# First feed-forward of a hybrid transformer layer, context rows: where the latent rows are asked for, how many weight pieces are under way, and where the position sums stand

## The chip, the cores and the metric

The program runs on one core of one Trainium2 chip. The metric is the device time of one execution in microseconds, a median of three runs. Five engines take part, each with its own stream of instructions that runs in order: TensorE (PE: matrix products; its weight loads are listed as PEld), VectorE (DVE), ScalarE (ACT), GpSimd (POOL) and SyncE (SP), whose queue asks for all the transfers between DRAM and SBUF that are spoken of here. An instruction that waits holds up everything behind it on its engine.

## The reference, cut to what matters

One layer over 1024 latent rows and 256 context rows of width 1024, all in float32. Both streams go through the same first feed-forward with their own shift, scale and gate; latents have grid positions added first:

```python
h = x + grid_pos_emb(rows)          # latents, 1024 rows
hc = ctx                            # context, 256 rows

def ffn_sublayer(h, shift, scale, gate, g, w_in, w_out):
    hn = modulate(rmsnorm(h, g), shift, scale)
    a, b = jnp.split(hn @ w_in, 2, axis=-1)      # w_in (1024, 2 * 2816)
    y = (jax.nn.silu(a) * b) @ w_out
    return h + 0.5 * gate[:, None, :] * y

h  = ffn_sublayer(h,  mods[0],   mods[1],   mods[2],   g_ffn1, w_ffn1_in, w_ffn1_out)
hc = ffn_sublayer(hc, mods_c[0], mods_c[1], mods_c[2], g_ffn1, w_ffn1_in, w_ffn1_out)
```

Behind it come a combined projection, a two-way recurrent mixing, a gating branch, a second feed-forward and a last norm. The change touches none of these.

## The kernel before, in words

Every float32 product is made of three: each operand is split into a rounded part (ACT, a cast) and the remainder (DVE, a subtraction), and PE adds up high·high, high·low and low·high.

The stage of interest is the first product of the context rows. The input weights `w1i` come as 44 pieces of 128 x 1024 (512 KB), two for each of the NF = 22 column groups f: piece 2f for `a`, 2f + 1 for `b`. PE works through a piece in 24 matmuls (8 slices of the width, 3 products each; listed as `pa` and `pb`, `L195`). After each odd f, four instructions make the gated product of two groups: silu on ACT (`sil`, `L1134`), the product with `pb` on DVE (`L1140`), a cast on ACT (`gc`, `L1142`) and the remainder on DVE (`L1143`); two stores put it away (`gcsp`, `L1145`).

Class `Weights` runs the pieces. `fetch()` asks for the next one into a `raw` tile (`L131`): of four in a row two use a pair of tiles of their own, and two use pages of a larger set. `load()` splits the oldest one asked for into an `hl` tile (cast `L158` on ACT, subtraction `L159` on DVE) and then asks for one more. There are five `hl` tiles, so a piece can be split only when PE is done with the piece five earlier. Eight pieces are asked for before the stage; `W.asked` is the newest.

Beside it the same loop prepares the latents for the stage behind it. They come as 16 tiles `h[tb][d]` of 128 x 512 (256 KB; two halves tb, eight slices d), asked for at `L1103`, two in each f from 1 to 8. For f from 2 to 9 the positions are added on DVE (`add_pos`, `L901`), and the squares are taken on ACT (`L219` for the first of each half, `L222`) and summed on DVE (`acc`, `L223`). At f = 10 come the norm of the latents (sums over the width on PE, `L228`; an inverse root in small DVE instructions, `L788` to `L800`; a diagonal, `L238` and `L239`; its broadcast on PE, `rb`, `L244`), then scaling in place (`L275` on DVE, `L276` on ACT) and splits of the scaled tiles (`fa`, later `fb` and `fc`, with differences at `L328`). From f = 13 on, weights of the next stage are asked for as well (`rawh`, `L385`) and summed (`L392`, `L393`). The next stage is a product of the latents with the same weights in seven-product form (`Gate`; PE `L429`, weights split into `ring` tiles).

Side work of this sort isn't issued where it is written: it is put into a list `todo` (`slow` does this with a price), and `pump`, called after each group of three matmuls, takes entries from it as credit allows.

A scheduler orders what is traced: it puts the instructions of each engine into one order when the program is built, by dependencies and its own idea of durations. `tc.issue_after(x)` binds what is traced inside it to stand behind instruction x if both are on the same engine. It makes no wait on the chip; it only fixes order. `behind(fn, ins)` wraps a function in such bounds. In the kernel before, each piece is asked for behind the one before it, and the rows of `h` behind `W.asked`, the newest piece asked for when the loop is at that f. The transfers that SP asks for also take turns with eight completion marks, so that one asked for waits until the one eight earlier has landed.

Of the kernel before, what the change touches and what calls it, by code (L numbers as in the profile page):

```python
# [55 lines left out]
def _build(ctx, tc, nc, a, out):  # L56
# [50 lines left out]
    class Weights:  # L107


        def __init__(self, order, name):  # L110
            self.c = ExitStack()
            self.pool = self.c.enter_context(tc.tile_pool(name=name, bufs=1, reuse_waits="tile"))
            self.order = deque(order)
            self.ready = deque()
            self.raws = deque()
            self.asked = None
            self.held = 0
            self.n = 0

        def fetch(self):  # L120
            n, i, w = self.order.popleft()
            src = a[n][i]
            if self.n % 4 < 2:
                raw = self.pool.tile([128, w], F32, name="raw", tag="raw", bufs=2)
            else:
                raw = hnp.tile([128, w], F32, name="raw", tag="pg1", bufs=8)
            self.n += 1
            with ExitStack() as es:
                if self.asked is not None:
                    es.enter_context(tc.issue_after(self.asked.ins))  # L130
                self.asked = nc.sync.dma_start(raw, src)  # L131
            self.raws.append((n, i, w, raw))

        def load(self):
            if not self.raws:
                self.fetch()
            n, i, w, raw = self.raws.popleft()
            hl = self.pool.tile([128, 2, w], F32R, name="hl", tag="hl", bufs=5)
            split(hl, raw)
            self.ready.append((n, i, hl))  # L140
            self.held += 1
            if self.order:
                self.fetch()

        def take(self, n, i):
# [11 lines left out]
    def split(hl, src):  # L157
        hi = S.copy(hl[:, 0, :], src)  # L158
        return hi, V.tensor_sub(hl[:, 1, :], src, hl[:, 0, :].bitcast(F32))  # L159

    def behind(fn, ins):

        def run():
            with ExitStack() as es:
                for i in ins:
                    es.enter_context(tc.issue_after(i.ins))
                fn()

        run.cost = COST(fn)
        return run  # L170
# [723 lines left out]
    def add_pos(tb, d, h=h, pos=pos):  # L894
        hv = h[tb][d].rearrange("p (r c) -> p r c", c=64)
        if d < 4:
            pv = pos[:, d * 16 + tb * 8:d * 16 + tb * 8 + 8].unsqueeze(2).to_broadcast([128, 8, 64])
        else:
            o = 64 + (d - 4) * 64
            pv = pos[:, o:o + 64].unsqueeze(1).to_broadcast([128, 8, 64])  # L900
        V.tensor_tensor(hv, hv, pv, ALU.add)  # L901
# [192 lines left out]
    def slow(fn, *args, cost=1024):  # L1094
        f = it(fn, *args)
        f.cost = cost
        todo.append(f)

    for f in range(1, NF):
        if f <= NKT:  # L1100
            with tc.issue_after(W.asked.ins):
                for tb in range(2):
                    nc.sync.dma_start(h[tb][f - 1], a["xT"][f - 1, :, tb * 512:(tb + 1) * 512])  # L1103
        if 2 <= f < 2 + NKT:
            if f - 2 < len(SIDE):
                slow(side, *SIDE[f - 2], 0)
            for tb in range(2):
                slow(add_pos, tb, f - 2)
                slow(n1[tb].sq, f - 2)
        if f == 2 + NKT:  # L1110
            todo.extend([n1[0].rstd, nop, n1[1].rstd, nop, n1[0].bcast, n1[1].bcast])
            for d in range(NKT):
                slow(n1[0].inplace, d, s0, b0)
                slow(A.F.early, fpage, 1 if d < 4 else 2, d % 4)
            for d in range(NKT):
                slow(n1[1].inplace, d, s0, b0)
        if f == 12:
            A.head()
        if f > 12:
            with tc.issue_after(W.asked.ins):  # L1120
                A.preload()
        if f == 1:
            pa, pb = pab
        else:
            if f % 2 == 0:
                pa, pb = mm_ps("pa"), mm_ps("pb")
            for pt, i in ((pa, 0), (pb, 1)):
                proj(pt[:, f % 2 * 256:f % 2 * 256 + 256], W.take("w1i", 2 * f + i), hnc, f % 2 == 0)
                W.done()
        if f % 2 == 0:  # L1130
            continue
        with ExitStack() as es:
            sil = t2("sil")
            S.activation(sil, pa, AF.Silu)  # L1134
            if f == NF - 1:
                flush()
                W.c.close()
                A.begin()
                es.enter_context(tc.issue_after(A.q.last[1].ins))
            V.tensor_mul(sil, sil, pb)  # L1140
            g = [t2("gc", F32R) for _ in range(2)]
            S.copy(g[0], sil)  # L1142
            V.tensor_sub(g[1], sil, g[0].bitcast(F32))  # L1143
        for y in range(2):
            nc.sync.dma_start(gcsp[f // 2, y].rearrange("p f c -> p (f c)"), g[y].bitcast(F32))  # L1145
# [1353 lines left out]
```

## Time and profile before

| what | value |
|---|---|
| median of 3 runs | 2636.53 us (2634.86 to 2637.92) |
| the profiled execution: its own time, its span | 2635.57 us, 2633.8 us |
| PE busy in the span | 2614.7 us (99%) |
| DVE, ACT, POOL busy | 1976.6 us (75%), 1206.5 us (46%), 75.0 us (3%) |
| granted TensorE clock | 0.998 |
| transfers | 449.07 MB, mean 171 GB/s |

The span runs from the first to the last instruction; 1.77 us of the execution's own time lie outside it. Matmuls overlap in the profile, so a busy PE says that it was never without work, not that it could do no more. The stage that the change touches lies between about 24 us (first matmul of the context product) and 161.7 us (the last one); the latents' product follows at once. In a row of the waits stand the waiting engine and line, who ended the wait, the total in us, how often, and the longest.

### The profile page before, as it was taken

How to read it: one execution, taken by the hardware profiler on the slowest of the kernel's cores; microseconds unless marked ns; L12 is line 12 of the kernel's file. 1: busy time of each engine (PE TensorE's matmuls, PEld its weight loads, DVE VectorE, ACT ScalarE, POOL GpSimd, SP SyncE). 2: the span in 40 equal slices, each digit the busy share in tenths (PEclk: the TensorE clock that was granted, in tenths of full speed). 3: DMA queues.
4: the chain of work that ended last, by engine and by line, in shares of the span. 5: the costliest groups of instructions: out<-in, count | busy, mean ns of one | idle time of the engine just before them, and what ended most of it. 6: DMA issues, size and time to landing. Idle time of an engine off the chain costs nothing.

```text
span 2633.8 us, 36017 instructions
## 1 busy us (share of the span) xinstructions
PE 2614.7 (99%) x12930; PEld 2214.2 (84%) x12930; DVE 1976.6 (75%) x3529; ACT 1206.5 (46%) x2170; POOL 75.0 (3%) x158
## 2 busy tenths in 40 slices
PE   9999999999999999999999999999999999999998
PEld 9988888888889878888888888888887888888887
DVE  6989678687989646787674878778799766665855
ACT  5754444444347525564443454333346444344433
POOL 0000000000000000000000002221000000000000
PEclk9999999999999999999999999999999999999999
DMA  9734345368577122256553566446441333337644
GB/s 341 267 137 146 125 150 175 124 234 301 177 268 264 66 80 92 104 187 194 191 184 104 172 205 237 162 154 203 136 150 47 128 136 124 112 125 281 200 159 179
DMA packets 192691, 449.07 MB, mean 171 GB/s; under 512 B 20096, under 2 KB 44160, under 8 KB 192512
## 3 DMA queue, kind: packets, MB, share of 16 engines
q1 hardware_dynamic: 192080, 446.38, 49.6%
q8 instruction: 102, 1.67, 0.3%
q14 instruction: 77, 0.63, 0.1%
q10 hardware_dynamic: 432, 0.39, 0.0%
HBM read 325.44 MB, written 121.32 MB: 170 GB/s over the span
## 4 chain that ended last, share of the span: by engine, by line
PE 91%; DMA 4%; DVE 2%; issue 2%; ACT 1%; SPq 0%; POOL 0%; POOLq 0%; ACTq 0%; DVEq 0%
PE qa L429 18%; PE pq L1462 17%; PE po L553 14%; PE qb L429 13%; PE pt L1946 6%; PE pr L1381 6%; PE po L2320 3%; PE pc L1248 2%; PE pn L2106 2%; PE pb L195 2%; PE pa L195 1%; PE pu L1782 1%; PE pkc L1441 1%; PE pn L2104 1%; PE pvc L1538 1%
## 5 line engine op out<-in xcount | busy, mean ns | idle before, releaser
L159 DVE TENSOR_TENSOR ring<-rawq,ring 128x512 fp32r<-128x512 f32 x408 | 280.9, 689 | 221.7 <-ACT ring L158 219.6
L553 PE MATMUL po<-gring,wring 128*128 128x512 f32 (+1 forms) x1896 | 423.5, 384 | 0.0
L553 PEld LDWEIGHTS po<-gring,wring 128*128 128x128 f32 x1896 | 349.5, 188 | 70.0
L158 ACT CAST ring<-rawq 128x512 fp32r<-128x512 f32 x408 | 253.5, 622 | 310.4 <-PE pq L1462 85.0
L429 PE MATMUL qa<-fc,ring 128*128 128x512 f32 x1056 | 252.8, 389 | 0.4 <-DVE fc L159 0.4
L429 PEld LDWEIGHTS qa<-fc,ring 128*128 128x128 f32 x1056 | 197.9, 188 | 42.7 <-DVE fc L159 0.8
L1462 PE MATMUL pq<-fc,ring 128*128 128x512 f32 x864 | 207.3, 392 | 0.0
L158 ACT CAST wring<-rw 128x512 fp32r<-128x512 f32 x154 | 95.8, 622 | 216.1 <-PE po L553 194.6
L1462 PEld LDWEIGHTS pq<-fc,ring 128*128 128x128 f32 x864 | 161.5, 188 | 32.9
L1946 PE MATMUL pt<-yp,ring 128*128 128x512 f32 x768 | 186.1, 396 | 0.0
L1946 PEld LDWEIGHTS pt<-yp,ring 128*128 128x128 f32 x768 | 144.2, 190 | 28.7
L159 DVE TENSOR_TENSOR wring<-rw,wring 128x512 fp32r<-128x512 f32 x154 | 105.6, 686 | 80.3 <-ACT wring L158 79.5
L1462 PE MATMUL pq<-fa,ring 128*128 128x512 f32 x576 | 141.9, 394 | 0.0
L1462 PE MATMUL pq<-fb,ring 128*128 128x512 f32 x576 | 136.8, 391 | 0.0
L429 PE MATMUL qb<-fb,ring 128*128 128x512 f32 x528 | 127.1, 390 | 0.7 <-DVE fb L159 0.4
L429 PE MATMUL qa<-fa,ring 128*128 128x512 f32 x528 | 127.1, 390 | 0.5 <-DVE ring L159 0.5
L429 PE MATMUL qa<-fb,ring 128*128 128x512 f32 x528 | 126.8, 390 | 0.0
L429 PE MATMUL qb<-fa,ring 128*128 128x512 f32 x528 | 126.5, 389 | 0.0
L1462 PEld LDWEIGHTS pq<-fb,ring 128*128 128x128 f32 x576 | 107.6, 188 | 22.4 <-issue 0.2
L429 PE MATMUL qb<-fc,ring 128*128 128x512 f32 x528 | 126.2, 389 | 0.0
L1462 PEld LDWEIGHTS pq<-fa,ring 128*128 128x128 f32 x576 | 106.9, 188 | 21.9 <-DVE ring L159 0.2
L429 PEld LDWEIGHTS qb<-fb,ring 128*128 128x128 f32 x528 | 98.8, 188 | 22.5 <-DVE fb L159 1.2
(384 smaller groups left out, 4686.0 us busy)
## 6 DMA issues: line engine op xcount, KB each, us to landing
fsp<-fhl SPq DMA_DIRECT2D x66, 512.0 KB, 2.8
gring<-fsp SPq DMA_DIRECT2D x66, 512.0 KB, 4.1
adapg<-in_w_ada_dram SPq DMA_DIRECT2D x112, 256.0 KB, 3.3
raw<-in_w1i_dram SPq DMA_DIRECT2D x44, 512.0 KB, 5.2
graw<-fsp SPq DMA_DIRECT2D x88, 256.0 KB, 3.6
rawq<-in_w1i_dram SPq DMA_DIRECT2D x38, 512.0 KB, 3.6
rawq<-in_w2i_dram SPq DMA_DIRECT2D x38, 512.0 KB, 3.5
fsp<-p SPq DMA_DIRECT2D x66, 256.0 KB, 2.1
```

The lines of the kernel that those rows point to most:

```text
L158: hi = S.copy(hl[:, 0, :], src)
L159: return hi, V.tensor_sub(hl[:, 1, :], src, hl[:, 0, :].bitcast(F32))
L195: T.matmul(pt, x, y, start=first and i == 0, stop=i == n - 1, skip_group_check=True)
L429: T.matmul(pt, hl[:, x, sl], pages[p][k][:, y, :], start=first and i == 0, stop=i == 11, skip_group_check=not first)
L553: T.matmul(pt[:, cs], w[:, x, sl], g[:, y, cs], start=grp and kp == 0 and i == 0, stop=kp == NFP - 1 and i == 2, skip_group_check=not grp)
L1248: T.matmul(pt, hl[d // 4][:, x, sl], g[:, y, :], start=f == 0 and d % 2 == 0 and i == 0, stop=f == NF - 1 and i == 2, skip_group_check=True)
L1381: T.matmul(self.pt[m], pg[:, x, sl], hl[:, y, :], start=first and k == 0 and i == 0, stop=k == 3 and i == 2, skip_group_check=not first)
L1441: T.matmul(self.cp[:, o:o + 256], hl[:, x, k * 128:(k + 1) * 128], hnc[kc][:, y, :], start=p == 1 and k == 0 and i == 0, stop=p in (2, 4) ...
L1462: T.matmul(pt, hl[:, x, k * 128:(k + 1) * 128], pg[k][:, y, :], start=first and k == 0 and i == 0, stop=k == 3 and i == 2, skip_group_chec ...
L1946: T.matmul(pt, hl[:, x, k * 128:(k + 1) * 128], pg[:, y, :], start=kh + k + i == 0, stop=kh == 1 and k == 3 and i == 2)
L2106: T.matmul(pn[:, 0:257], qi[:, c_, :], self.C[d][:, c_, :], start=False, stop=c_ == 1)
L2320: T.matmul(pt, hl[:, x, k * 128:(k + 1) * 128], FO[p][k][:, y, :], start=first and k == 0 and i == 0, stop=k == 3 and i == 2, skip_group_c ...
```

## The change

Three edits in one stage. (1) `load()` asks for another piece only while fewer than three are under way, so that the eight asked for at first run down to two before the ninth (piece 8) is asked for; before, each split asked for one more. (2) The rows of `h` for a given f are placed behind piece 5 + 2f (`W.log` keeps every request), where they were placed behind the newest piece. (3) Each addition of positions is placed behind the remainder (DVE subtraction) of the newest piece split at the time when `pump` takes it from the list; before, it had no such bound.

```diff
 class Weights:
+            self.log = []
...
                 self.asked = nc.sync.dma_start(raw, src)
+            self.log.append(self.asked)
             self.raws.append((n, i, w, raw))
...
             hl = self.pool.tile([128, 2, w], F32R, name="hl", tag="hl", bufs=5)
-            split(hl, raw)
+            self.low = split(hl, raw)[1]
             self.ready.append((n, i, hl))
             self.held += 1
-            if self.order:
+            if self.order and len(self.raws) < 3:
                 self.fetch()
...
     for f in range(1, NF):
         if f <= NKT:
-            with tc.issue_after(W.asked.ins):
+            with tc.issue_after(W.log[5 + 2 * f].ins):
                 for tb in range(2):
                     nc.sync.dma_start(h[tb][f - 1], a["xT"][f - 1, :, tb * 512:(tb + 1) * 512])
         if 2 <= f < 2 + NKT:
             if f - 2 < len(SIDE):
                 slow(side, *SIDE[f - 2], 0)
             for tb in range(2):
-                slow(add_pos, tb, f - 2)
+                slow(lambda d=f - 2, tb=tb: behind(lambda: add_pos(tb, d), [W.low])())
                 slow(n1[tb].sq, f - 2)
```

No instruction is added or taken away on any engine; the orders change. Line numbers from 117 on are one higher in the changed kernel, and two higher from 133 on. Three places show it.

First place: SP's queue and ACT's stream from the point where piece 4 is asked for to about piece 15. SP before (`raw` is a weight piece, `h` a tile of latents, `gcsp` a store of the gated product):

```order
L1089 DMA cst<-in_cst_dram 128x384
L131 DMA raw<-in_w1i_dram 128x1024 x9
L1145 DMA gcsp<-gc 128x512
L131 DMA raw<-in_w1i_dram 128x1024 x3
L1145 DMA gcsp<-gc 128x512
L131 DMA raw<-in_w1i_dram 128x1024
L1103 DMA h<-in_xT_dram 128x512 x4
L131 DMA raw<-in_w1i_dram 128x1024 x2
```

SP after the change:

```order
L1091 DMA cst<-in_cst_dram 128x384
L132 DMA raw<-in_w1i_dram 128x1024 x4
L1105 DMA h<-in_xT_dram 128x512 x2
L132 DMA raw<-in_w1i_dram 128x1024 x4
L1105 DMA h<-in_xT_dram 128x512
L1147 DMA gcsp<-gc 128x512
L1105 DMA h<-in_xT_dram 128x512
L1147 DMA gcsp<-gc 128x512
L132 DMA raw<-in_w1i_dram 128x1024 x2
L1105 DMA h<-in_xT_dram 128x512 x2
L132 DMA raw<-in_w1i_dram 128x1024 x2
```

The first two tiles of `h` stand behind piece 7 where they stood behind piece 16, and pieces 12 to 15 stand behind both stores of f = 1, where piece 12 stood ahead of both and 13 to 15 between them.

ACT before, from the silu of f = 1 to the silu of f = 3 (`hl` is the cast of a piece, 8 to 15 here; `acc` and `sq` are squares of `h`):

```order
L1134 ACTIVATE sil<-pa 128x512
L158 CAST hl<-raw 128x1024 x2
L1142 CAST gc<-sil 128x512
L158 CAST hl<-raw 128x1024 x5
L219 ACTIVATE acc<-h 128x512
L158 CAST hl<-raw 128x1024
L219 ACTIVATE acc<-h 128x512
L222 ACTIVATE sq<-h 128x512
L1134 ACTIVATE sil<-pa 128x512
```

ACT after the change:

```order
L1136 ACTIVATE sil<-pa 128x512
L160 CAST hl<-raw 128x1024 x2
L1144 CAST gc<-sil 128x512
L160 CAST hl<-raw 128x1024
L221 ACTIVATE acc<-h 128x512 x2
L160 CAST hl<-raw 128x1024
L224 ACTIVATE sq<-h 128x512
L160 CAST hl<-raw 128x1024
L1136 ACTIVATE sil<-pa 128x512
```

The silu of f = 3 stands three casts earlier: behind piece 12's, where it stood behind piece 15's.

Second place: PE around the norm of the latents (`p` are the sums over the width, `rb` the broadcasts; pieces 22 to 25). Before:

```order
L195 MATMUL pb<-hnc,hl 128x256 x21
L228 MATMUL p_1233<-ones,acc 128x1 x4
L195 MATMUL pb<-hnc,hl 128x256 x3
L195 MATMUL pa<-hnc,hl 128x256 x11
L228 MATMUL p_1279<-ones,acc 128x1 x4
L195 MATMUL pa<-hnc,hl 128x256 x13
L195 MATMUL pb<-hnc,hl 128x256 x21
L244 MATMUL rb<-diag,onesr 128x512
```

After the change:

```order
L197 MATMUL pa<-hnc,hl 128x256 x18
L230 MATMUL p_1223<-ones,acc 128x1 x4
L197 MATMUL pa<-hnc,hl 128x256 x6
L197 MATMUL pb<-hnc,hl 128x256 x6
L230 MATMUL p_1269<-ones,acc 128x1 x4
L197 MATMUL pb<-hnc,hl 128x256 x18
L197 MATMUL pa<-hnc,hl 128x256 x12
L246 MATMUL rb<-diag,onesr 128x512
L197 MATMUL pa<-hnc,hl 128x256
L246 MATMUL rb<-diag,onesr 128x512
L197 MATMUL pa<-hnc,hl 128x256 x11
L197 MATMUL pb<-hnc,hl 128x256 x2
```

The first sum stands in piece 22, 18 of 24 matmuls in, where it stood in piece 23, 21 in: 27 matmuls earlier. The second follows after 12 matmuls instead of 14, and the first broadcast after 30 more instead of 34; two more `rb` follow behind these rows.

Third place: DVE from the last piece's split to the first weights of the latents' product (`ring`). Before, behind the split `hl` and one `L392`:

```order
L1140 TENSOR_TENSOR sil<-sil,pb 128x512
L393 TENSOR_TENSOR rawh<-rawh 128x512
L392 TENSOR_TENSOR s1s<-rawh 128x512
L1143 TENSOR_TENSOR gc<-sil,gc 128x512
L393 TENSOR_TENSOR rawh<-rawh 128x512
L159 TENSOR_TENSOR fb<-h,fb 128x512
L328 TENSOR_TENSOR h<-h 128x512 x3
L159 TENSOR_TENSOR fb<-h,fb 128x512 x3
L328 TENSOR_TENSOR h<-h 128x512 x3
L159 TENSOR_TENSOR fb<-h,fb 128x512 x3
L328 TENSOR_TENSOR h<-h 128x512
L159 TENSOR_TENSOR ring<-rawh,ring 128x512 x4
```

After the change, from the same split on:

```order
L161 TENSOR_TENSOR hl<-raw,hl 128x1024
L161 TENSOR_TENSOR fb<-h,fb 128x512
L1142 TENSOR_TENSOR sil<-sil,pb 128x512
L330 TENSOR_TENSOR h<-h 128x512 x2
L1145 TENSOR_TENSOR gc<-sil,gc 128x512
L161 TENSOR_TENSOR fb<-h,fb 128x512 x2
L330 TENSOR_TENSOR h<-h 128x512 x3
L161 TENSOR_TENSOR fb<-h,fb 128x512 x3
L330 TENSOR_TENSOR h<-h 128x512 x2
L161 TENSOR_TENSOR fb<-h,fb 128x512 x2
L161 TENSOR_TENSOR ring<-rawh,ring 128x512 x4
```

The sums of the next stage's weights (`L392`, `L393`) have moved ahead of the last split: 17 instructions of this size stand between it and the first `ring`, where 20 stood. From the first instructions of the latents' product on, all five orders are the same again.

## The prediction

> **What bounds the kernel now.** I read the head of the page first, then a table by stage, then PE's waits, then the rows around each of them.
>
> ```profile
> span 2633.8 us, 36017 instructions
> PE 2614.7 (99%) x12930; PEld 2214.2 (84%) x12930; DVE 1976.6 (75%) x3529; ACT 1206.5 (46%) x2170; POOL 75.0 (3%) x158
> ```
>
> ```profile
> core 0: us, PE busy (x) PEld busy (x) DVE busy (x) ACT busy (x) POOL busy (x), PEclk, DMA share, GB/s
> 40.20:163.30 123.10, 121.98 (x1003) 120.60 (x1002) 112.66 (x172) 83.58 (x120) 0.00 (x0) 1.00 0.76 262
> 40.20:100.24 60.04, 59.77 (x496) 59.36 (x495) 52.88 (x67) 37.66 (x49) 0.00 (x0) 1.00 0.90 309
> ...
> 112.90:161.70 48.80, 48.80 (x408) 48.74 (x407) 47.49 (x66) 36.91 (x55) 0.00 (x0) 1.00 0.64 223
> ```
>
> ```profile
> PE qa L429 <- DVE ring L159: 0.5, 1, 0.5
> PE p L228 <- DVE acc L223: 0.3, 1, 0.3
> PE pa L195 <- ACT sil L1134: 0.3, 1, 0.3
> ```
>
> PE is busy for 2614.7 of 2633.8 us: 19.1 us of the whole span are PE without work. The orders differ only between about 40 us and the start of the latents' product, and there (first row by stage) PE lacks 123.10 - 121.98 = 1.12 us. The three waits listed last are PE's waits in that stretch, and they are all of it: 0.50, 0.34 and 0.27 us, as rows below tell more closely. So the change can gain 1.1 us here, 0.04% of the time, and no more; whatever it does to DVE, ACT and the transfers counts only if PE comes to wait for it. DVE is the next fullest engine: 52.88 of 60.04 us while the latents come in, 47.49 of 48.80 us at the end.
>
> **How far ahead the weights are.** Next: what would a late piece have to eat up first? The first rows are single instructions (start, duration, engine, line, what ended an idle time before them), the next are SP's requests, then come a wait of SP, two groups of DVE (count, busy us, mean ns), and two landing times (request to arrival, shortest, median and longest), for `h` and for pieces.
>
> ```profile
> 38.97 1.21 DVE L159 TENSOR_TENSOR hl<-raw,hl 128x1024 fp32r<-128x1024 f32 x1
> ...
> 45.86 0.68 DVE L1140 TENSOR_TENSOR sil<-sil,pb 128x512 f32<-128x512 f32 x1
> ...
> 48.11 0.69 DVE L1143 TENSOR_TENSOR gc<-sil,gc 128x512 fp32r<-128x512 f32 x1 [0.37 <-ACT gc L1142]
> ...
> 53.83 3.04 PE L195 MATMUL pa<-hnc,hl 128*128 128x256 f32 x24
> 54.08 1.05 ACT L158 CAST hl<-raw 128x1024 fp32r<-128x1024 f32 x1 [1.82 <-PE pb L195]
> ...
> 65.78 3.14 PE L195 MATMUL pa<-hnc,hl 128*128 128x256 f32 x24 [0.27 <-ACT sil L1134]
> ```
>
> ```profile
> 31.82 1.61 SPq L131 DMA_DIRECT2D raw<-in_w1i_dram  x2
> ...
> 45.97 0.33 SPq L131 DMA_DIRECT2D raw<-in_w1i_dram  x1
> ...
> 51.30 0.42 SPq L1145 DMA_DIRECT2D gcsp<-gc  x1
> ...
> 56.78 1.85 SPq L1103 DMA_DIRECT2D h<-in_xT_dram  x4
> ...
> 76.86 0.85 SPq L1145 DMA_DIRECT2D gcsp<-gc  x2
> ```
>
> ```profile
> SPq L131 <- DVE hl L159: 36.6, 15, 5.5
> ```
>
> ```profile
> L159 DVE TENSOR_TENSOR hl<-raw,hl 128x1024 fp32r<-128x1024 f32 x40 | 48.4, 1218 | 5.9 <-ACT hl L158 5.9
> ...
> L901 DVE TENSOR_TENSOR h<-h,pos 128x512 f32<-128x512 f32 x16 | 10.7, 686 | 2.5 <-DMA h<-in_xT_dram 2.5
> ```
>
> ```profile
> DMA to landing us min/median/max: 4.0/5.4/7.5
> ```
>
> ```profile
> DMA to landing us min/median/max: 3.3/5.2/11.7
> ```
>
> A piece occupies PE for 2.88 us (24 matmuls at 0.12 us from start to start; the 3.04 us of a row contain the overlap with the next). The matmuls at 53.83 us are piece 8; the cast at 54.08 us is piece 12's, and it waited for PE to leave piece 7, whose `hl` tile it takes. So splits run four pieces, 11.5 us, ahead of PE, and it is tiles that hold them back here, not transfers. SP's rows tell that the seven requests ahead stand in the program's text only: SP waited for DVE 15 times, 36.6 us in sum, because a request needs an older piece to be split out of its tile. The rows of `h` stand behind that, and the first went out at 56.78 us.
>
> **The change part by part.**
>
> *Requests for pieces (44 DMAs, moved, none added).* In the changed order a group of four pieces, 2f + 10 to 2f + 13, stands behind the two stores of an odd f. The second store of f = 1 needs the remainder of `gc`, done at 48.80 us; it now has one addition and one split ahead of it (0.69 + 1.22 us at most), so it goes at about 50.7 us, against 51.30. Piece 12 is asked for right behind it instead of at 45.97; with 5.2 us to land, 1.05 for its cast and 1.22 for its subtraction it is split at about 58.2, or 64.7 with the longest landing. PE takes it up at 65.78. For f = 5 even the stores from 76.86 us on, as before, leave enough: PE comes to piece 20 eight pieces (23.0 us) after piece 12, at 88.8 us, and 76.86 + 5.2 + 1.05 + 1.22 = 84.3 us, 4.4 us to spare. With silu placed nearer to its matmuls, as it now is, the stores go some 7 us earlier (end of piece 11 at 65.5 us, four instructions of 0.6 to 0.7 us and about one more of each kind between them), and the spare is near 12. I cost the part at 0, hidden by those 4 to 12 us. The page "DMA: Bandwidth & Descriptors" of the Trainium skill (Rules for kernel authors) advises to issue a DMA early and to wait on it late; taken alone it speaks against three pieces instead of seven, and by it the sum would come out above the time before. The trace agrees only as far as requests were early in time, and here SP itself held them back.
>
> *Rows of h (16 DMAs of 256 KB, the first moved ahead by nine pieces).* They take 4.0 to 7.5 us to land, and the first is now asked for behind piece 7, whose request ends the row at 31.82 us: at about 34.4 us. The addition that needs it stands behind the product that ends at 46.5 us. Its transfer lies ahead of piece 8's, which can't be asked for anyway before piece 4 is split, at 40.18 us. Cost 0.
>
> *Additions behind a remainder (16 on DVE).* It only fixes order; 16 additions are 10.7 us of DVE before and after. Behind a waiting addition stand DVE's splits, and PE feels those only once four pieces are used up. DVE was without work for 7.16 of the 60.04 us in which the latents came in, and 2.5 of them it waited in an addition for its tile. Cost 0, hidden by the same lead.
>
> *Silu of f = 3 (-0.27).*
>
> ```profile
> 61.12 0.69 DVE L901 TENSOR_TENSOR h<-h,pos 128x512 f32<-128x512 f32 x1 [1.86 <-DMA h<-in_xT_dram]
> ...
> 61.85 0.63 ACT L219 ACTIVATE acc<-h 128x512 f32<-128x512 f32 x1 [0.96 <-DVE h L901]
> ...
> 65.15 0.58 ACT L1134 ACTIVATE sil<-pa 128x512 f32<-128x512 f32 x1
> ```
>
> PE's piece 12 (65.78 us) needs the bank that this silu reads. The silu stood behind squares of `h`, which waited for DVE, which waited for the landing. It now stands behind piece 12's cast, near 57 us: 8 us before it is needed. The wait goes, and late next would be piece 13's bank, free with DVE's product right behind. Bounds: -0.27 to 0; I take the whole, as 8 us are far from none.
>
> *Sums of the norm (-0.34).*
>
> ```profile
> 99.84 0.68 DVE L223 TENSOR_TENSOR acc<-acc,sq 128x512 f32<-128x512 f32 x1
> ...
> 100.58 1.05 PE L228 MATMUL p<-ones,acc 128*128 128x1 f32 x8 [0.34 <-DVE acc L223]
> ...
> 103.25 0.95 PE L228 MATMUL p<-ones,acc 128*128 128x1 f32 x8
> ...
> 108.23 0.50 PE L244 MATMUL rb<-diag,onesr 128*128 128x512 f32 x1
> ...
> 112.50 0.39 PE L244 MATMUL rb<-diag,onesr 128*128 128x512 f32 x1
> ```
>
> The first sum now comes 27 matmuls earlier (3.2 us) and without the 0.27 and the 0.34: at about 96.7 us. Its `acc` stands behind piece 25's split, whose tile is free when PE leaves piece 20 (65.5 + 9 x 2.88 = 91.4 us); cast, subtraction and sum of 1.05 + 1.22 + 0.68 end at about 94.4, two us early. If DVE were not so free but as late as before, the queue ahead would be shorter by one split and one addition, at their spacing 1.15 + 0.60 us: 100.52 - 1.75 = 98.8, and PE would wait 2.1. Bounds: -0.34 to +1.8; I take -0.34, since DVE has the 7.16 us without work to spare.
>
> *Broadcasts (+0.4).* From the second sum to the first broadcast PE now has 30 matmuls instead of 34, and to the last 46 instead of 61, so 0.5 to 1.8 us less time to cover a chain of small instructions on DVE and ACT. Before, no broadcast waited, and how near it was the trace does not show. DVE's scaling of the first tile now also stands ahead of the second diagonal, and it waits for the first broadcast. Bounds 0 to +1.75 (the same distance from the second sum kept: 112.50 - 103.25 = 9.25 us against 7.5); I take +0.4, nearer to 0, because the four rows of before were covered.
>
> *Start of the latents' product (-0.50).*
>
> ```profile
> 147.53 1.05 ACT L158 CAST hl<-raw 128x1024 fp32r<-128x1024 f32 x1 [1.83 <-PE pa L195]
> ...
> 149.34 1.22 DVE L159 TENSOR_TENSOR hl<-raw,hl 128x1024 fp32r<-128x1024 f32 x1
> ...
> 162.51 2.49 DVE L159 TENSOR_TENSOR ring<-rawh,ring 128x512 fp32r<-128x512 f32 x4
> ...
> 163.25 7.78 PE L429 MATMUL qa<-fa,ring 128*128 128x512 f32 x33 [0.50 <-DVE ring L159]
> ```
>
> DVE is without a pause from piece 43's split at 149.34 us to the first `ring` at 162.51: 20 instructions between them, (162.51 - 149.34 - 1.14) / 20 = 0.60 us each. Now 17 stand there, so `ring` is ready 1.8 us earlier, and 0.50 are needed. The split itself stays where it is, since its cast waits for PE. Bounds: -0.50 to 0; I take the whole.
>
> Sum: -0.27 - 0.34 + 0.4 - 0.50 = -0.7 us. The profiled execution took 2635.57 us (span 2633.8 and 1.77 outside), so it would take 2634.9; it lies 0.96 below the median of the three runs, 2636.53, and I predict on the median: 2635.8 us. Nothing in the rows behind the stage moves with it except by this shift.
>
> **Rivals.** The bound for a difference is 0.2% or 5.3 us, about what a measurement of this kernel can tell from no change.
>
> *Weights late (slower).* Place: the stores, behind which each group of four pieces now stands on SP. If every landing took the 11.7 us of the longest row instead of 5.2, and stores came as late as at 76.86, each of the 8 groups from piece 12 to 43 would miss PE by 11.7 - 5.2 - 4.4 = 2.1 us: 17 us, 2653. It decides from a spare of zero, and passes 5.3 us when a group is 0.7 us late on average. For it: stores and pieces share one queue, and the transfers run at 309 GB/s with 0.90 of their time taken. Against it: the median landing, and less is under way at a time, not more. This is also where the rule of the Trainium skill would lead ("DMA: Bandwidth & Descriptors", Rules for kernel authors: issue early, wait late). Chance 4%.
>
> *DVE held up by an addition (slower).* An addition in front of a split waits for its tile of `h`; PE feels it once DVE has stood for more than four pieces less one cast and one split, 11.5 - 2.3 = 9.2 us. The longest landing of `h` is 7.5 us, so one late tile alone can't do it; two in a row could, for about 6 us: 2642. Chance 2%.
>
> *Nothing happens.* The pair of `raw` tiles limits requests as before, the order holds PE as near to full as it was, and new waits of a few tenths replace the old: 2636.5, up to 2640.1 if both upper bounds above came true and the waits at silu and `ring` stayed (1.8 + 1.75). Chance 40%.
>
> *Faster by more than 0.2%.* PE would have to lose 5.3 us of waits, and has 1.12 in the stage. Only waits far behind could add to it, and their order stays. Chance 1%.
>
> **How the numbers follow.** My forecast, a gain of some tenths, has 53%; with "nothing happens" 93% lie within 0.2%, 6% slower, 1% faster. The range: below, the whole of 1.12 us gained, less the 1.7 us by which the lowest of the three runs lies under their median: 2633.7. Above, both upper bounds, 2640.1; it leaves out the two slower cases.
>
> **What would show it.** Right: no wait of PE on `sil` near 65 us and on `ring` near 162; the first `h` asked for near 34 us; the first sum near 97 us; casts of pieces still ended by PE, not by a transfer; PE's busy time in the stretch equal to it within a microsecond. Wrong: rows of PE waiting on `hl`, casts waiting on `raw` for several us in each group, DVE waiting on `h` in rows of more than 5 us. The forecast falls if PE's lead of four pieces is used up anywhere.

## The result, and the profile after

| | kernel before | changed kernel |
|---|---|---|
| median of nine executions each, us | 2634.86 (2632.81 to 2639.8) | 2629.42 (2626.28 to 2633.13) |
| ratio, 95% interval | | 0.9977 (0.9967 to 0.9987) |
| profiled execution, its own time, us | 2635.57 | 2628.53 |
| mean of all executions of this study, us | 2633.73 (120) | 2630.28 (21) |

Forecast were 2635.8 us, no change that can be measured. The first measurement lies 6.4 us below that: 1.7 us because nine executions of the kernel before have a lower median than the three that were shown, and 4.7 us because the change gave 5.4 us where 0.7 were forecast. Over all executions the gain is 3.45 us (2.3 to 4.5 by resampling), 0.13%: still some five times the forecast, but less than the first measurement. That pools measurements made at different times, between which the mean of the kernel before alone moves from 2632.2 to 2635.6 us; where both kernels ran beside each other, the means differ by 6.2 us the first time and 3.0 us the second.

The head of the page after, to be laid beside the prediction's first rows: PE is busy for 3.7 us less, though it does the same 12930 matmuls, and without work for 15.8 us where it was 19.1.

```profile
span 2626.8 us, 36007 instructions
PE 2611.0 (99%) x12930; PEld 2211.0 (84%) x12930; DVE 1975.7 (75%) x3529; ACT 1205.5 (46%) x2170; POOL 76.8 (3%) x158
```

By stage, the changed kernel (the first row is the stretch of the change, the second the recurrent mixing stage near the kernel's middle; columns as in the prediction's table, the seventh is the granted clock of PE):

```profile
40.20:163.30 123.10, 122.27 (x1006) 121.24 (x1005) 114.74 (x176) 83.48 (x120) 0.00 (x0) 1.00 0.74 259
...
1580.00:1810.00 230.00, 227.00 (x1264) 199.41 (x1262) 177.05 (x513) 93.78 (x247) 59.84 (x126) 1.00 0.55 183
```

and the mixing stage of the kernel before:

```profile
1580.00:1810.00 230.00, 223.93 (x1227) 195.87 (x1225) 171.93 (x495) 92.58 (x244) 57.26 (x124) 0.99 0.53 178
```

In the stage of the change PE lacks 0.83 us instead of 1.12; in the mixing stage, which no line of the change touches, it did 37 matmuls more in the same 230 us. Start times of identical matmuls tell the same: the changed profile is 1.14 us ahead at the fourth matmul of the latents' product, 0.3 us behind at 1570 us, and 7.0 us ahead at the end of the execution, with 6.6 us won between 1583 and 1664 us.

Now the places of the forecast, in the changed kernel: SP's first and last request for `h`; the silu; the first sum; the first `ring`.

```profile
33.67 0.81 SPq L1105 DMA_DIRECT2D h<-in_xT_dram  x2
...
83.32 1.42 SPq L1105 DMA_DIRECT2D h<-in_xT_dram  x2
```

```profile
57.86 0.59 ACT L1136 ACTIVATE sil<-pa 128x512 f32<-128x512 f32 x1
```

```profile
96.24 0.69 DVE L225 TENSOR_TENSOR acc<-acc,sq 128x512 f32<-128x512 f32 x1
...
96.98 1.05 PE L230 MATMUL p<-ones,acc 128*128 128x1 f32 x8 [0.83 <-DVE acc L225]
```

```profile
160.87 2.50 DVE L161 TENSOR_TENSOR ring<-rawh,ring 128x512 fp32r<-128x512 f32 x4
```

PE's waits for silu and `ring` are gone; the sum waits, 0.83 us. And the last request for `h`, of which the prediction says nothing, moved as well: in the kernel before it was made 9 us later:

```profile
92.31 1.71 SPq L1103 DMA_DIRECT2D h<-in_xT_dram  x2
```

In the mixing stage of the kernel before, PE pauses for `kl` (the low part of the transposed keys), and the clock granted to it is halved for 3.41 us right behind, and once more at 1661.66:

```profile
1586.25 0.39 PE L1782 MATMUL pu<-wvh,kh 128*128 128x258 f32 x1 [2.45 <-DVE kl L2086]
```

```profile
1583.16:1586.57 3.41, 0.96 (x7) 0.73 (x6) 3.38 (x5) 2.28 (x5) 1.51 (x2) 1.00 1.08 373
...
1586.57:1589.98 3.41, 3.41 (x11) 2.72 (x10) 1.58 (x6) 1.03 (x3) 0.11 (x1) 0.50 1.04 404
1661.66:1665.07 3.41, 3.41 (x10) 2.67 (x9) 2.50 (x6) 3.41 (x10) 0.00 (x0) 0.50 0.26 98
```

PE is busy through both windows, so by an estimate from these rows each costs half of its 3.41 us, 1.7 us. The changed profile has neither the pause nor the windows: 2.4 + 2 x 1.7 = 5.8 us, about the gain that is not in the stage. Is that the change's doing?

### The profile page after: what moved, and what is told of

Read it like the earlier page. It is cut to its first block, busy times and chain, and to the rows that moved or that the text cites. A ratio compares the mean times of both kernels' runs of the same rounds, so it can differ in the third digit from the quotient of the medians.

```text
span 2626.8 us, 36007 instructions
## 1 busy us (share of the span) xinstructions
PE 2611.0 (99%) x12930; PEld 2211.0 (84%) x12930; DVE 1975.7 (75%) x3529; ACT 1205.5 (46%) x2170; POOL 76.8 (3%) x158
## 4 chain that ended last, share of the span: by engine, by line
PE 91%; DVE 2%; issue 2%; DMA 1%; ACT 1%; POOL 0%; SPq 0%; POOLq 0%; DVEq 0%; ACTq 0%
PE qa L431 18%; PE pq L1464 17%; PE po L555 15%; PE qb L431 13%; PE pt L1948 6%; PE pr L1383 5%; PE po L2322 3%; PE pc L1250 2%; PE pn L2108 2%; PE pb L197 1%; PE pu L1784 1%; PE pa L197 1%; PE pkc L1443 1%; PE pn L2106 1%; PE pvc L1540 1%
```

## Experiments: does the gain behind the stage belong to the change?

**Both kernels once more, and both delayed.** The delay repeats the first matmul of the latents' product:

```
+  [T.matmul(pt, hl[:, 0, 0:128], pages[p][0][:, 0, :], start=True, stop=True) for _ in range(5)]
```

> The kernel before, unchanged, against itself. Question: does its profile again hold what the first one held in the recurrent mixing stage, PE's wait of 2.4 us for kl near 1583 us and two windows of 3.4 us at half clock (near 1587 and 1662 us, about 1.7 us each)? Theory A (the wait is a fixed property of this program: a transfer of yraw that lands 2 us late behind others): the wait is there again, ratio 1.000 within 0.1%. Theory B (an accident of one execution): wait and windows are gone or lie elsewhere, the time scatters over 2632 to 2640 us as before, ratio 1.000 within 0.1%.

> The changed kernel, unchanged, a second measurement. Theory A (a fixed gain downstream): ratio 0.9977 again, within 0.1%, about 2629 us, and the profile again without the wait for kl and without half-clock windows before the end. Theory B (1.1 us of waits removed in the stage, the other 4 us an accident of the nine runs): ratio 0.9992 to 1.000, 2633 to 2635 us.

> The changed kernel with five extra matmuls of 0.236 us (the first matmul of the latents' product repeated, 1.18 us on PE) at 161 us, so that all behind it starts about when it starts in the kernel before. Theory C (the gain far behind follows the time of arrival there): the wait for kl and the time of before come back, about 2634 to 2635 us, ratio 0.9997. Theory A (the gain downstream does not hang on the 1.1 us): 1.2 us more than the changed kernel, 2630.6 us, ratio 0.9982.

> The kernel before with the same five extra matmuls. Theory C: the stage far behind moves by another 1.2 us, and its cost by an amount that can be of either sign, up to some 4 us; the time differs from before + 1.2 us by more than 1 us. Theory A: 1.2 us more than before, 2636.1 us, ratio 1.0004 within 0.1%.

Measured: 2632.78 (ratio 0.9998, 0.9987 to 1.0009), 2630.47 (0.9988, 0.9977 to 0.9999), 2633.32 (0.9998, 0.9986 to 1.0009) and 2633.94 us (0.9999, 0.9989 to 1.0009). The profiles decide more than the ratios. PE's waits in the second profile of the kernel before, then of the changed kernel:

```profile
PE pu L1782 <- DVE C L1783: 3.1, 3, 1.4
PE pu L1782 <- DVE kl L2086: 1.6, 1, 1.6
PE p L228 <- DVE acc L223: 1.3, 1, 1.3
```

```profile
PE pu L1784 <- DVE C L1785: 4.6, 4, 2.6
PE pu L1784 <- DVE kl L2088: 1.7, 1, 1.7
```

The kernel before had no half clock this time but at its very end, where every profile has one; the changed one had the pause for `kl` and a window at half clock (at 1731.87 us). Its two profiles differ by 5.9 us (spans of 2626.8 and 2632.7), all of it from the mixing stage. So neither pause nor window belongs to one of the kernels: theory B holds for the windows, the pause came again in the kernel before but in the changed one too, and the 5.8 us above are an accident of two executions. The gain itself repeated, at 3 us; its ratio lies between the ranges of the two theories. The five extra matmuls cost the changed kernel 3.1 us and the kernel before 0.2 by the means, where 1.2 each had been laid in, and the ratio of the delayed changed kernel is where theory C put it. The traces tell more of it: from the first matmul of the latents' product to the same one near 600 us, the kernel before took 438.3 us in both profiles and 438.7 with the delay, the changed one 437.4 and 437.6, and 438.7 with it. So the kernel before pays only 0.4 us, because the extra matmuls stand where PE would wait for `ring`; of the 3.1 us in the changed kernel this accounts for 1.2. To see about the rest, the delay was doubled.

> The changed kernel with ten extra matmuls (2.36 us) at 161 us. Theory L (the time does not hang on when PE arrives in later stages; the 3.1 us that the five extra matmuls cost, and the 0 that they cost in the kernel before, are scatter): the changed kernel + 2.4 us, 2632.5 us, ratio 0.9995 within 0.1%. Theory C (the time of arrival matters): 2635 us or more, or 2630.5 or less.

2633.34 us (1.0004, 0.9995 to 1.0013), by the means 2.8 us (1.4 to 4.1) above the changed kernel and the kernel of the next paragraph, taken together, for 2.36 us laid in: theory L. That twice the delay cost no more than the single one shows what a difference of 1 us between two such medians is worth here.

**The pause for kl taken away.** The late splits go behind `kh` and `kl` on ACT and DVE:

```
-  page_splits(yb, lds.pop(t, ()))
+  behind(lambda: page_splits(yb, lds.pop(t, ())), hd.low)()    # hd.low: the last kh cast and kl subtraction
```

> The changed kernel, and in the recurrent mixing stage the splits of the late ybsp pages stand behind the casts and subtractions that make kh and kl, on ACT and DVE, instead of in front of them. PE waited for kl there near 1583 us in six of seven executions (0.4 to 2.4 us), and half clock of 3.4 us followed in some. Theory K (this wait and the half clock behind it are what scatters between executions and cost the rest): no wait for kl, no half clock before the end, some 1.5 to 3 us less than the changed kernel, 2627.5 to 2629 us, ratio 0.9978. Rival (the late splits hold up the loop behind, dn and hm stand behind them): the time stays at 2630 us or grows, and PE waits for C or dn instead.

2630.25 us (0.9991, 0.9982 to 1.0). The wait for `kl` is gone; PE's waits in the mixing stage are these, and one window at half clock came all the same, at 1727.87:

```profile
PE pu L1784 <- DVE C L1785: 2.6, 3, 1.9
PE pu L1784 <- DVE wvl L1779: 0.5, 1, 0.5
```

Theory K falls on the time. Its eleven executions lay within 3.2 us, which looked like the scatter explained, but with a lower limit on requests besides, twelve lay within 7.7 us (last experiment). Part of that scatter can be read from the granted clock, which is on record for each execution. Of 111 executions of the kernel before, those with a mean clock of 0.999 (it is given to a thousandth) took 2631.4 us in the mean (44 of them), with 0.998 2634.2 (49), with 0.997 2636.6 (16), with 0.996 2642.1 (2); a thousandth of the span is 2.6 us, and the steps are 2.4 to 5.5. At the same clock the changed kernel is 2.9 us faster at 0.999 (2628.5, nine executions) and 2.6 us at 0.998 (2631.6, twelve). What starts half clock in one execution and not in another, and what makes executions of equal clock differ (the 7.7 us above are such), stays open.

## Experiments: where in the stage it comes from

To look at the stage with less of that scatter, kernels were ended behind the gate half of the latents' product, near 600 us.

> The kernel before, ended after the gate half of the latents' product (near 610 us): everything behind it is left out and the output is zeros. It is the base for the next three and shows how much the first 610 us scatter by themselves. Theory L (the stage of the change is quiet, the scatter of 2629 to 2643 us comes from behind): runs within 1.5 us of each other, PE waiting 1 to 2.5 us for silu, sums and ring between 40 and 165 us. Rival (the scatter is everywhere): a spread of 3 us or more.

> The changed kernel, ended at the same place. Theory L (the change's whole effect is in its stage; PE's waits there were 1.1, 2.2 and 2.5 us in three executions of before, delayed start left aside, and 0.8, 0 and 0 in three of the changed order): 1.7 to 2.5 us less than the cut kernel before. Theory M (1.1 us in the stage, as the first trace alone says, and 2 us or more behind it by some other arrival): 1.1 us less or under. Theory N (all of the 3.2 to 5.4 us measured on the whole kernel arises here): 3.2 us less or more.

> The cut kernel before with one edit alone: no request for a piece while three or more are under way. Theory H (what helps is that h is asked for 9 pieces earlier, so that additions and squares don't hold up silu and sums): this edit alone leaves the first h behind piece 10 or later, gives under 0.7 us. Rival F (what helps is that splits, silu and sums stand in another order, which this edit alone brings too): 1.2 us or more.

> The cut kernel before with one edit alone: rows of h asked for behind the fixed pieces 7, 9, 11 ... instead of behind the newest request. Theory H: most of the gain of the three edits, 1.2 us or more. Rival F: under 0.7 us.

The edits: all three in e6; one line each in e7 and e8 (which also keeps the list `W.log`):

```
-            if self.order:
+            if self.order and len(self.raws) < 3:                  # e7
```

```
-            with tc.issue_after(W.asked.ins):
+            with tc.issue_after(W.log[5 + 2 * f].ins):             # e8
```

The third edit alone leaves the order of instructions on every engine as it was and was not run. Measured: 597.4, 594.71, 594.52 and 604.13 us. The limit on requests alone brings the whole gain, the early request for `h` alone costs 6.7 us. Theory H was wrong on both, on the early request even in sign; rival F's numbers hold, its reason is looked at below. PE's waits between 30 and 120 us with the early request alone; then DVE's addition, and PE's first sum:

```profile
PE p L228 <- DVE acc L223: 4.8, 1, 4.8
PE pa L195 <- DVE hl L159: 1.6, 1, 1.6
```

```profile
42.10 0.69 DVE L901 TENSOR_TENSOR h<-h,pos 128x512 f32<-128x512 f32 x1 [4.55 <-DMA h<-in_xT_dram]
```

```profile
102.90 1.87 PE L228 MATMUL p<-ones,acc 128*128 128x1 f32 x8 [4.83 <-DVE acc L223]
```

```profile
100.18:113.83 13.65, 10.93 (x51) 10.94 (x52) 7.94 (x30) 3.11 (x4) 0.00 (x0) 0.50 0.42 143
```

Two mechanisms show. An addition that waits 4.55 us for its tile stands in front of a split, and PE misses that split for 1.6 us: the rival "DVE held up by an addition"; one late tile was enough for it, not two. And the first sum, which now stands 27 matmuls earlier in PE's row (all variants with an edit on `h` or requests have it there), waits 4.8 us, and half clock follows for 13.65 us, of which PE works through 10.93 and so loses 5.5. The sum waits because the last rows of `h` come no earlier than before; requests that wait for a free tile stand ahead of them on SP:

```profile
91.66 1.08 SPq L1103 DMA_DIRECT2D h<-in_xT_dram  x2
```

With the limit alone these rows are asked for 11.5 us earlier:

```profile
80.15 1.24 SPq L1103 DMA_DIRECT2D h<-in_xT_dram  x2
```

**Pairs, and the pause filled.**

> The cut kernel before with two edits, fewer pieces under way and h behind fixed pieces; additions are not tied to a remainder. On DVE two additions then stand ahead of a split again near 42 us. Theory D (an addition that waits for its tile of h in front of a split stops PE: 4.55 us of waiting and 1.6 us of PE in the run with the early requests alone): PE waits about 1.6 us for hl near 43 us, and the time is 1.5 us or more above the cut kernel with fewer pieces alone, 596 us or more. Rival Q (what went wrong there was the queue of seven requests, not the additions): 594.5 us and no wait for hl.

> The cut kernel before with two edits, h behind fixed pieces and additions behind the newest remainder; up to seven pieces asked for ahead as before. Theory D: no wait of PE for hl near 43 us, the 4.8 us wait for the sums near 98 us gone or under 1 us, 594.5 to 596.5 us. Rival Q (the seven requests ahead delay h or pieces whatever the additions do): PE waits 2 us or more for hl or sums, above 599 us.

> The cut kernel before with the early requests for h alone (604.1 us, where PE paused 4.8 us for the first sums near 98 us and then ran at half clock for 13.65 us), plus 20 matmuls on constants (some 4.8 us) that PE does in place of that pause. Theory G (the pause itself cost 4.8 us at most, the half clock that followed it 6.8 us): no half clock after 98 us, 597 to 598 us. Rival (the half clock comes from something else, or the pause only moves behind the filling): 602 us or more.

> The changed kernel cut at 610 us, but no request while two or more pieces are under way. Theory R (the limit acts by how early the last rows of h are asked for: 92 us and later with no limit, 80 to 84 with three): the last h is asked for at 84 us or earlier, the first sum waits for nothing or under 1 us, 594 to 595 us as with three. Rival (fewer pieces under way come too late for PE): casts wait for raw, PE waits 2 us or more for hl, 597 us or more.

> The changed kernel cut at 610 us, but no request while five or more pieces are under way. Theory R: the last h is asked for between those with three (83 us) and those with no limit and the same two other edits (87 us), the first sum, at the same place in PE's row, waits 1 to 2.6 us, and half clock may follow; 595.5 to 599 us. Rival (the limit only works through the order of instructions, which is the same here as with three): 594.7 us and no wait for the sum.

The filling is one line in `sums`, once:

```
+  [T.matmul(p4[:, 0:128], ones, ones, start=True, stop=True) for _ in range(20)]
```

All of the cut kernels, from their profiles (us; medians over four or five executions, of before over eight):

| cut kernel | last `h` asked for | first sum begins | it waited | PE's wait for `hl` | half clock behind it | time |
|---|---|---|---|---|---|---|
| before (two profiles) | 91.9, 92.9 | 99.7, 100.8 | 0, 0.4 | 0 | 0 | 597.1 |
| limit 3 | 80.2 | 96.1 | 0 | 0 | 0 | 594.5 |
| limit 3, early h | 83.7 | 97.3 | 0 | 0.6 | 0 | 595.3 |
| all three edits (limit 3) | 83.1 | 96.2 | 0 | 0 | 0 | 594.7 |
| the same, limit 2 | 75.2 | 96.2 | 0 | 0 | 0 | 593.7 |
| the same, limit 5 | 83.5 | 96.1 | 0 | 0 | 0 | 594.1 |
| early h, additions tied, no limit | 86.5 | 98.9 | 2.6 | 0 | 10.24 | 599.4 |
| early h alone | 91.7 | 102.9 | 4.8 | 1.6 | 13.65 | 604.1 |
| early h alone, pause filled | 93.7 | 103.7 | 0.6 | 1.4 | 0 | 600.2 |

Read down the second column: with the sum at its earlier place, PE's wait grows with the time of the last request, from nothing at 83.7 us to 4.8 us at 91.7 (the 0.8 us in the first profile of the whole changed kernel came another way, told under the sums below). The rows of DVE show why. Without the limit (early h, additions tied) an addition near the end waits for its tile, and the sums of squares stand behind it:

```profile
94.59 0.69 DVE L901 TENSOR_TENSOR h<-h,pos 128x512 f32<-128x512 f32 x1 [2.01 <-DMA h<-in_xT_dram]
```

With a limit of five, DVE waits for `h` between 60 and 100 us but once:

```profile
DVE h L903 <- DMA h<-in_xT_dram: 0.2, 1, 0.2
```

So for the first sum the limit works through the last rows of `h`, and is saturated at five pieces: theory R expected a wait there and was wrong, since with five the last request is no later than with three; its rival had 594.7 us and no wait right. The first sum stands at the same place in PE's order with a limit and without (early h, additions tied; the second sum and the broadcasts stand a little later without, and DVE and ACT differ too), so the earlier place alone gives no gain: with the last rows at 86.5 us the kernel is 2.3 us slower than the one before. For the sum, rival F is out. For the other two waits it is not: PE's wait for `ring` is gone in every one of these kernels but the one before, with a limit or without, and that for silu in all but the one with the filled pause (0.4 us). That goes with the new orders; by which of their moves, and how far through the times of the requests, isn't separated here. Tying additions to a remainder takes away the wait for `hl` (1.6 to 0, and 0.6 to 0), so theory D has the place right, but not the sizes: 0.6 us of wait and 0.75 us of time where it expected 1.6 and 1.5. The longer wait, for the sum, is rival Q's.

The filled pause confirms theory G's mechanism and misses its number. No half clock follows now:

```profile
98.45 4.62 PE L226 MATMUL p<-ones 128*128 128x128 f32 x40
...
103.71 1.05 PE L228 MATMUL p<-ones,acc 128*128 128x1 f32 x8 [0.64 <-DVE acc L223]
```

The time fell by 3.9, not 6.8 us: part of the 13.65 us had lain in the pause itself (5.5 lost, not 6.8), and the filling ended 0.8 us later than the pause did. The 0.8 us that still lack lie within the scatter of these executions.

**Back on the whole kernel, and the better version.**

> The whole kernel before with the one edit that no piece is asked for while three or more are under way; h is still asked for behind the newest request, additions have no extra order. In the kernel cut at 610 us this edit alone measured 594.5 us against 597.4 before and 594.7 with all three edits. Theory L (the whole effect is in the stage, and this edit is all of it): ratio 0.9990 (2.7 us), within 0.1%, the same as the changed kernel. Rival S (the early requests for h bring something behind 610 us that this edit does not): ratio 0.9995 or above.

> The kernel before cut at 610 us, a second time. Theory L: median again 597 to 598 us, 2.5 to 3.5 us above the cut kernels with a limit; PE waits 1 to 2.5 us between 40 and 165 us, half clock only at the end. Rival (the first four runs were high by chance): under 596 us. If half clock stands behind the wait for the sums near 100 us, the part of the gain that PE's waits do not cover is explained by it.

> The changed kernel with the limit at two pieces instead of three (593.7 against 594.7 us in the cut kernel) and kh and kl ahead of the late splits (no wait for kl, executions within 3.2 us of each other instead of 10). If the two add up: 2629 to 2629.5 us, ratio 0.9982, scatter as small as with kh and kl first alone. If nothing is left in the smaller limit: 2630.2 us, ratio 0.9987 to 0.9991.

The limit alone: 2630.98 us (0.9989, 0.998 to 0.9997), the same as the changed kernel (0.9988 in its second measurement); theory L. The cut kernel before a second time: 596.71 us, 0.3 under what theory L expected and 0.7 above the rival's bound; eight executions together 597.1, from 595.4 to 598.5; the cut kernels with the limit alone and with all edits lie 2.4 us (1.6 to 3.2) below their mean. Both profiles of it fell on the shortest execution of their four, and show no half clock before the end. Of the eight only the longest, 598.5 us, has a lower granted clock (0.989; the others 0.992 to 0.995, as with the limit), so half clock explains at most a small part of what PE's waits leave over. Limit 2 with `kl` first: 2629.22 us (0.9981, 0.9972 to 0.9989), as expected if the two add up, but with a scatter that was not; the lowest of all, 1.2 us below the changed kernel by the means, with an interval from 2.7 below to 0.4 above it.

## Why the prediction was wrong

- **"So the change can gain 1.1 us here ... and no more": the step that failed first.** It took PE's idle time, of one execution, for what the waits cost. First, one execution: over five profiles of the kernel before PE waited there 1.1, 2.2, 2.5, 1.1 and 1.3 us; over six with all three edits (plain, delayed, cut, `kl` first) 0.8 once and otherwise nothing. That is 1.5 us, not 0.7. Second, a wait cost more than its row says. The start of the latents' product, before and after:

```profile
161.73 1.02 PE L429 MATMUL qa<-fa,ring 128*128 128x512 f32 x3
```

```profile
161.41 2.91 PE L431 MATMUL qa<-fa,ring 128*128 128x512 f32 x12
```

Before, the fourth matmul starts at 163.25, 1.52 us behind the first; in the changed kernel three starts take 0.70 us. The wait is listed with 0.50 because the profile lets the third matmul last until 162.75. By the 41st matmul 0.95 us were lost (10.04 against 9.09). From the first matmul of the context product to the 201st of the latents' product, the profile that the prediction read took 184.17 us, where three profiles with the edits and no wait took 182.25 in the mean: 1.9 us, from the very execution in which idle time gave 1.1. Four profiles of each order (two whole and two cut; three whole and one cut) differ by 1.9 us in the mean as well. The cut kernels say 2.4 us (1.6 to 3.2); the 0.5 between them no profile shows, and it is within the interval.
- **Requests, and rows of `h` (0 and 0): mis-sized.** Their own times came true (first `h` at 33.67 against 34.4, the silu at 57.86 against 57, no wait of PE for weights). The sign "casts of pieces still ended by PE, not by a transfer" did not hold: in the changed kernel's profile casts waited five times for their piece, 6.9 us in sum, against three times and 2.7 us before; the lead hid it from PE but for the sum below. I followed the first rows of `h`, and it was the last ones, 9 us earlier, that let the sum stand 27 matmuls earlier without a wait. That the limit alone brings the whole gain, and that the early request is a loss by itself, is not in the prediction. The Trainium skill's rule ("DMA: Bandwidth & Descriptors", Rules for kernel authors: issue early, wait late) points the wrong way here: of a shared queue, fewer early requests for weights gave 2.4 us; with more of them `h` stands behind requests that wait for tiles.
- **Silu (-0.27) and `ring` (-0.50): right that they go, mis-sized.** Both waits are gone in every profile with the three edits; `ring` came 1.64 us earlier, against 1.8. Over five executions of before they were 0.5 and 0.6 us by the rows, and `ring` 0.95 from start to start in the profile that was read.
- **Sums (-0.34): the place right (96.98 against 96.7), the wait not in the profile after (0.83), where the accumulation ended at 96.93 and not at 94.4;** right in the other five, where nothing waits. In the one that waits, DVE stood 2.86 us behind a cast whose piece came late, and was then without work for only 0.42 us up to the sum, so the spare that the prediction counted on was gone:

```profile
69.81 1.05 ACT L160 CAST hl<-raw 128x1024 fp32r<-128x1024 f32 x1 [2.96 <-DMA raw<-in_w1i_dram]
```

- **Broadcasts (+0.4): nothing waited;** the cover held.
- **The rival "DVE held up by an addition"** asked for more than 9.2 us of standing DVE, and so for two late tiles. In the kernel with the early request alone one wait of 4.55 us near 42 us was enough: the lead of four pieces, read at 54 us, was not there at that time.
- **"Nothing in the rows behind the stage moves with it except by this shift": not refuted.** The 5.9 us that the two profiles show there come and go in one kernel. 3.45 us (whole), 2.6 to 2.9 us (whole, at equal clock) and 2.4 us (cut) agree within their intervals; up to some 2 us behind the stage are not excluded.
- **The chances.** "Faster by more than 0.2%" got 1%, because the waits seen in one execution could not pay for 5.3 us. Over all executions that holds (0.13%), but nine executions with a scatter of 2 to 3 us each can say 0.23%: the range allowed for the low end of three executions before, 1.7 us, and for no scatter of those after.

## What to carry to other kernels

When a limit on requests moves, follow the last transfer behind it on the queue to its consumer, not only the first; what stands behind a request that waits for a free tile is late by that wait. Take a wait's size from start to start of the matmuls around it, and from several executions, before it caps a gain; take no gain from a difference in a stage that the change doesn't touch until an unchanged kernel has been run again. If time must be read to 2 us in a kernel that scatters by 10, end it behind the stage in question.

## What the runs showed of the clock

A pause of PE that is shorter than one window of the clock gate can halve its clock for several. In the cut kernel with early `h`, tied additions and no limit, PE paused for 2.62 us; the window of 3.41 us up to 98.26, in which it had worked 1.42, was followed by three windows at half clock, though PE was busy for nearly all of them:

```profile
98.88 1.87 PE L228 MATMUL p<-ones,acc 128*128 128x1 f32 x8 [2.62 <-DVE acc L223]
```

```profile
94.85:98.26 3.41, 1.42 (x12) 1.21 (x11) 3.41 (x6) 2.12 (x3) 0.00 (x0) 1.00 0.45 136
```

```profile
98.26:108.50 10.24, 9.62 (x45) 9.62 (x46) 5.62 (x25) 1.12 (x2) 0.00 (x0) 0.50 0.44 161
```

With 4.83 us it was four windows; in the mixing stage, behind windows with 0.96 and 1.66 us of work, one each; a wait of 1.3 us for the same sum, in the kernel before, had none. Laid over all twenty profiles, from the start of the context product to some 50 us before the end, the grid of these windows shows a border near half a window: the eight in which PE was busy for 1.66 us or less were all followed by half clock (in one of them it held already), and of the eleven with 1.75 to 2.28 us one was (1.79). The Trainium skill ("TensorE: Matmul & The Clock Gate", Part 1) gives the window of 3413 ns, which the trace shows to the digit (10.24 is three of them), and says that half clock comes after at least one idle window and full clock after at least one busy one; here a window that was not idle was enough, and half clock lasted for three windows that were mostly or wholly busy.
